# Reordering the first loads, the memory loads and the first branch steps of a one-core hybrid decoder layer

## The chip, the core and the metric

The kernel runs on one core of a Trainium2 chip (trn2). The metric is the device time of one execution in microseconds (us). The engines are PE (TensorE; PEld is its weight load), DVE (VectorE), ACT (ScalarE), POOL (GpSimd) and SP (SyncE, which here only issues DMAs). ACT and POOL can issue DMAs as well.

## What is computed

One decoder layer on 256 tokens of width 1024, in f32. The reference, cut to what matters:

```python
h = rms_norm(x, g_mix)
u_ssm, q, k, v, qi, ki, wi, qm, gates = split(h @ w_in)
km, vm = split(rms_norm(mem, g_mem) @ w_mem_kv)
y_ssm = s5_branch(u_ssm, ...)          # diagonal state space layer, gelu, glu
y_dsa = dsa_branch(q, k, v, qi, ki, wi, pos)   # indexer, top 64 keys per query, attention
y_mem = memory_branch(rms_norm(qm), rms_norm(km), vm)   # cross-attention to mem
merged = g_s * (y_ssm @ w_up_ssm) + g_d * (y_dsa @ w_up_dsa) + g_m * (y_mem @ w_up_mem)
x = x + merged @ w_out
x = x + hier_moe(rms_norm(x, g_ffn), ...)   # 32 experts, two per token
```

## The kernel before, in words

There are two stages. The **dense stage** holds everything up to the output projection. The **expert stage** goes through all 32 experts, each with three weight matrices of 2 MiB.

The dense stage is a list of jobs, each a product of all tokens with a weight matrix of up to 512 columns. A job is cut into *quarters* of two 128-row pieces of the weight. There are 70 quarters; `job` (from L208) appends them in the order of the calls: u (quarters 0 to 3), a (4 to 7), q (8 to 11), then the memory jobs km (12 to 15), qm (16 to 19), vm (20 to 23), the six gates (24 to 47), the up-projections of the memory, of the attention, the GLU, the up-projection of the state space branch, and the output projection. In the code u feeds the state space branch, a and q feed the attention, km, qm and vm the cross-attention.

For each quarter q:

- `load_quarter` (L222 to L227) issues the weight load on SP into one of four raw places; the load of quarter q + 4 therefore has to wait until quarter q is split.
- `split` (L229 to L243) writes the weight as a sum of two fp32r parts: `S.copy` on ACT (L241) makes the high part and `V.tensor_tensor` on DVE (L242) the low one. Quarter 0 is split in two halves, the others in one piece. Then it loads quarter q + 4. The main loop calls `split(q + 2)`.
- `product` (L245 to L264) issues 12 matmuls, each high x high, high x low and low x high (L257, L258, L259), in two parts of six. The last quarter of a job ends with the job's evacuation (`scaled`, L268 to L271, is the one for u, a, q, km, qm, vm: ACT scales by the reciprocal root mean square rx or rm).

The activations are split in the same way by `split_T` (L350 to L354): ACT makes the scaled high part (L353), DVE the low part (L354), in eight pieces of 256 columns, for x from `xT_raw` and for the memory from `mT_raw`.

The three branches are Python generators, "a" (`attention`), "s" (`ssm`) and "m" (`memory`). The table STEPS (L40) has one entry for each half of a quarter, and each letter in it lets that generator issue its next step. A generator that needs a job's result yields the job; its letters then wait until the job is done. `finish` (from L1001) runs a generator until it ends or meets such a wait. "m" may not start before `load_memory` has been called.

The order in which the code is traced is not the final one. A list scheduler with a timing model puts the instructions of each engine, and the DMA issues of SP, in an order of its own; program order is its priority, and `tc.high_priority()` lifts what stands in it (the splits and quarter loads do). Each engine then runs its list strictly in order.

In the kernel before, all first loads are issued by SP: g8 (the norm gains, L193), x^T in three pieces (L194, L332, L334), the quarters, the two halves of x by tokens (L337), `early` (constants, L383), `ssm_bc` (state space matrices, L1064 at q == 1), the positions (L1066, L1067 at q == 2). `load_memory` (L342 to L348) is called at q == 6; it issues both memory loads, memT and mem, of 1 MiB each. Two copies of one column (L345, L346) from u's result tie these loads to the evacuation of job u.

The experts' weights go through a ring of places in SBUF. Most of these places hold data of the dense stage first, and `feed` (L972) issues an expert's load on SP as soon as its place has been given up.

Of the kernel before, what the change touches and what calls it, by code (L numbers as in the profile page):

```python
# [15 lines left out]
AF = mybir.ActivationFunctionType  # L16
# [22 lines left out]

STEPS = ("||s|s|s||sa|a|saa||s|ss|s|s|mm|mm|samm|amm|samm|amm|sa|a|sa|a|sa|a|sa|a|sa|a|sa|a|sam|am|sam|a|sa|a|"  # L40
         "sa|a|sam|am|sam|a|sa|a|sa|a|sam|a|sam|a|sam|a|sam|a|sam|a|sam|a|sam|a|sam|a|sam|a|sam|a|sam|a|sam|a|"
# [30 lines left out]
def hybrid_kernel(ctx: ExitStack, tc: tile.TileContext, A: dict, out: bass.AP):  # L72
# [15 lines left out]
    g8 = pool.tile([128, 2, 8], F32, name="g8")  # L88
# [103 lines left out]

    SP.dma_start(g8, A["g8"])  # L193
    SP.dma_start(xT_raw[:, 0:2], A["xT"][:, 0:2])  # L194

    warm = sl(24, 0, 512).bitcast(BF16)
    G.memset(warm, 0.0)

    S.activation(warm[:, 512:513], warm[:, 0:1], AF.Copy, scale=1.0)
    wps = at()  # L200
# [28 lines left out]
    def split(q):  # L229
        if q >= len(quarters):  # L230
            return
        j, i = quarters[q]
        load_quarter(q)
        w = j["w"]
        src = raw(q).rearrange("p k w -> p (k w)")
        new(SPL[q % 3], F32R)
        hi, lo = (sl(SPL[q % 3], 1024 * n, 2 * w) for n in range(2))
        j["w2"][i] = [v.rearrange("p (k w) -> p k w", k=2) for v in (hi, lo)]
        with tc.high_priority():
            for c in ((slice(0, w), slice(w, 2 * w)) if q == 0 else (slice(0, 2 * w),)):  # L240
                S.copy(hi[:, c], src[:, c])  # L241
                V.tensor_tensor(lo[:, c], src[:, c], hi[:, c], ALU.subtract)  # L242
            load_quarter(q + 4)  # L243
# [64 lines left out]
    Jm_ = dict()  # L308
    for n in ('km', 'qm', 'vm'):
        Jm_[n] = job(n, *(dict(km=(mT, halves(A["w_km"]), 512, scaled(toks[0], rm)), vm=(mT, halves(A["w_vm"]), 512, scaled(vm, rm)),  # L310
                               qm=(hT, halves(A["w_qm"]), 512, scaled(toks[2], rx)))[n]))
# [18 lines left out]

    load_quarter(0)
    SP.dma_start(xT_raw[:, 2:4], A["xT"][:, 2:4])  # L332
    load_quarter(1)
    SP.dma_start(xT_raw[:, 4:8], A["xT"][:, 4:8])  # L334
    load_quarter(3)
    for tt in range(2):
        SP.dma_start(x_tok[:, tt], A["x"][128 * tt:128 * tt + 128])  # L337
    posr, posc = sl(23, 256, 256).bitcast(I32), sl(23, 512, 2).bitcast(I32)
    bre, bim, cre, cim = (sl(21, 256 * i, 256, g=16, h=16) for i in range(4))

    mem_there = dict(done=False)
    def load_memory():  # L342
        mem_there["done"] = True

        S.copy(mT_raw[:, 0, 0:1], toks[0][:, 1, 0:1])  # L345
        S.copy(mem_tok[:, 0, 0:1], toks[0][:, 1, 0:1])  # L346
        for dst, src in ((mT_raw, A["memT"]), (mem_tok, A["mem"].rearrange("(t p) d -> p t d", p=128))):
            SP.dma_start(dst, src)  # L348

# [30 lines left out]
    for n_, _ in enumerate(split_T(hT, xT_raw, g8[:, 0])):  # L380
        if n_ in (1, 3):
            split(n_ // 2)
    SP.dma_start(early, A["early"])  # L383
    with tc.high_priority():
# [458 lines left out]

    def memory():
        sumsq(rm, mem_tok)
        yield
        inv_sqrt(rm, D)
        yield
        yield from split_T(mT, mT_raw, g8[:, 1])
        for J, tok, dst, g in ((Jkm, toks[0], kmT, "gkm"), (Jqm, toks[2], qmT, "gqm")):  # L850
            yield J
# [198 lines left out]
    for q in range(len(quarters)):  # L1050
        j, i = quarters[q]
        if j is Jkm and i == 0:
            finish(mmt)
# [8 lines left out]
        split(q + 2)  # L1062
        if q == 1:
            SP.dma_start(sl(21, 0, 1024), A["ssm_bc"])  # L1064
        if q == 2:
            SP.dma_start(posr, A["pos_row"])  # L1066
            SP.dma_start(posc, A["pos_col"])  # L1067
        if q == 6:
            load_memory()
        for part in range(2):  # L1070
            product(q, part)
            steps(STEPS[2 * q + part])
# [419 lines left out]
```

## Time and profile before

| | |
|---|---|
| median of three runs | 732.78 us (731.33, 732.78, 732.97) |
| profiled execution | 733.47 us |
| its span in the trace | 731.70 us |
| around the span | 1.77 us |
| PE busy | 581.6 us, 79% |
| DVE busy | 308.0 us, 42% |
| ACT busy | 211.5 us, 29% |
| moved by DMA | 246.78 MB, mean 337 GB/s |

The shares are means over two stages that have little in common; they have to be read stage by stage. A time in the trace is counted from the start of the span.

### The profile page before, as it was taken

To read this page: it belongs to the slowest core of one execution; us is meant where nothing else is said; L and a number is where in the kernel's file an instruction comes from. 1 tells how busy PE (TensorE), PEld (TensorE's weight loads), DVE (VectorE), ACT (ScalarE), POOL (GpSimd) and SP (SyncE) were. 2 spreads that over 40 slices of the span, in tenths; PEclk is the share of its full clock that TensorE was granted. 3 is DMA by queue.
4 is the path that set the end of the run, shared out by engine and by line. 5 is a ranking of instruction groups with operands and counts; after the bars stand their busy time and mean duration, and the time that the engine had idled before them with its cause. 6 is when DMAs were issued, how large, how long until landed. Compare 5 with 4: busy or idle time off the path is not lost.

```text
span 731.7 us, 12785 instructions
## 1 busy us (share of the span) xinstructions
PE 581.6 (79%) x5284; PEld 374.3 (51%) x5284; DVE 308.0 (42%) x772; ACT 211.5 (29%) x426; POOL 77.5 (11%) x122
## 2 busy tenths in 40 slices
PE   8889999999998999888676685495577668469765
PEld 4677787786876786444343252252233324234423
DVE  5999999999574755222120021021111012001102
ACT  6776764648743452111100001000000000000002
POOL 2722201001022001202020020001002002000000
PEclk9999999999999999999996799789879789789989
DMA  8874334436757979999999999999999999999992
GB/s 313 317 217 143 125 118 135 144 118 227 276 175 286 320 299 402 428 425 419 431 424 422 430 428 422 428 427 421 429 426 425 427 426 421 429 426 425 420 409 105
DMA packets 31358, 246.78 MB, mean 337 GB/s; under 512 B 3904, under 2 KB 4544, under 8 KB 15936
## 3 DMA queue, kind: packets, MB, share of 16 engines
q1 hardware_dynamic: 30352, 244.87, 83.4%
q8 instruction: 43, 0.70, 0.4%
q0 software_dynamic: 512, 0.53, 0.3%
q10 hardware_dynamic: 432, 0.52, 0.2%
q14 instruction: 19, 0.16, 0.1%
HBM read 244.33 MB, written 1.05 MB: 335 GB/s over the span
## 4 chain that ended last, share of the span: by engine, by line


## 5 line engine op out<-in xcount | busy, mean ns | idle before, releaser
L1267 PE MATMUL w<-arena 128*32 128x256 f32 x1088 | 125.1, 456 | 43.0 <-DMA arena<-w_up 31.0
L1267 PE MATMUL w<-s,arena 128*32 128x256 f32 x960 | 111.8, 439 | 30.7 <-DMA s<-w_up 29.6
L258 PE MATMUL pj<-s,s 128*128 128x512 f32 (+1 forms) x280 | 112.5, 402 | 4.8 <-DVE s L242 4.8
L257 PE MATMUL pj<-s,s 128*128 128x512 f32 (+1 forms) x280 | 110.0, 405 | 7.0 <-ACT s L241 3.4
L259 PE MATMUL pj<-s,s 128*128 128x512 f32 (+1 forms) x280 | 110.3, 397 | 0.1
L1267 PEld LDWEIGHTS w<-arena 128*32 128x32 f32 x1088 | 55.5, 130 | 90.0 <-DMA arena<-w_up 37.1
L242 DVE TENSOR_TENSOR s<-arena,s 128x1024 fp32r<-128x1024 f32 (+2 forms) x71 | 87.0, 1230 | 21.5 <-ACT s L241 20.9
L241 ACT CAST s<-arena 128x1024 fp32r<-128x1024 f32 (+2 forms) x71 | 72.7, 1029 | 47.3 <-PE pj L259 27.6
L1267 PEld LDWEIGHTS w<-s,arena 128*32 128x32 f32 x960 | 50.5, 125 | 69.0 <-DMA s<-w_up 35.8
L1225 POOL TENSOR_SCALAR s<-early,s 128x32 f32<-128x32 f32 x64 | 32.3, 522 | 350.0 <-PE w L1231 295.6
L1324 DVE COPY arena<-w 32x256 f32<-32x256 f32 x62 | 25.9, 418 | 91.4 <-PE w L1319 78.2
L1324 ACT COPY arena<-w 32x256 f32<-32x256 f32 x62 | 22.5, 364 | 143.7 <-DVE arena L1324 143.7
L257 PEld LDWEIGHTS pj<-s,s 128*128 128x128 f32 x280 | 52.4, 189 | 21.8 <-ACT s L241 6.7
L258 PEld LDWEIGHTS pj<-s,s 128*128 128x128 f32 x280 | 53.1, 190 | 18.8 <-DVE s L242 8.5
L1305 DVE TENSOR_TENSOR early<-w,early 64x256 f32<-64x256 f32 x16 | 6.8, 428 | 126.9 <-ACT early L1304 126.9
L259 PEld LDWEIGHTS pj<-s,s 128*128 128x128 f32 x280 | 53.0, 190 | 10.5 <-DVE s L696 0.5
L1304 ACT ACTIVATE misc<-w 64x256 f32<-64x256 f32 x16 | 6.0, 375 | 137.0 <-PE w L1267 137.0
L1319 PE MATMUL w<-s,s 128*32 128x256 f32 x544 | 34.8, 397 | 10.4 <-DVE s L1310 6.1
L1319 PE MATMUL w<-arena,s 128*32 128x256 f32 x448 | 32.2, 434 | 9.5 <-DMA arena<-w_down 6.0
L1304 ACT ACTIVATE early<-w 64x256 f32<-64x256 f32 x16 | 6.0, 377 | 115.6 <-PE w L1267 115.6
L1305 DVE TENSOR_TENSOR misc<-w,misc 64x256 f32<-64x256 f32 x16 | 6.8, 426 | 72.6 <-ACT misc L1304 72.6
L1260 DVE TENSOR_TENSOR arena<-w,misc 128x256 f32<-128x256 f32 x32 | 12.1, 420 | 57.1 <-PE w L1257 57.1
(307 smaller groups left out, 690.0 us busy)
## 6 DMA issues: line engine op xcount, KB each, us to landing
arena<-w_up SPq DMA_DIRECT2D x15, 2048.0 KB, 29.5
arena<-w_gate SPq DMA_DIRECT2D x13, 2048.0 KB, 29.5
arena<-w_down SPq DMA_DIRECT2D x12, 2048.0 KB, 30.7
s<-w_down SPq DMA_DIRECT2D x12, 2048.0 KB, 31.9
s<-w_gate SPq DMA_DIRECT2D x11, 2048.0 KB, 34.3
s<-w_up SPq DMA_DIRECT2D x9, 2048.0 KB, 34.2
s<-w_up SPq DMA_DIRECT2D x13, 1024.0 KB, 27.1
arena<-w_g SPq DMA_DIRECT2D x24, 512.0 KB, 3.9
```

The costliest lines, as they stand in the source:

```text
L241: S.copy(hi[:, c], src[:, c])
L242: V.tensor_tensor(lo[:, c], src[:, c], hi[:, c], ALU.subtract)
L257: PE.matmul(ps, lhsT=lh, rhs=hi[:, k], start=kt == 0, stop=False)
L258: PE.matmul(ps, lhsT=lh, rhs=lo[:, k], start=False, stop=False)
L259: PE.matmul(ps, lhsT=ll, rhs=hi[:, k], start=False, stop=kt == j["kts"] - 1)
L1225: G.tensor_scalar(dst[:, tt, :], iota[:, 0:CAP], col[:, tt:tt + 1], fac[:, tt:tt + 1], ALU.is_equal, ALU.mult)
L1260: V.tensor_tensor(xe[:, h], xg[:, k:k + 2], b_(gff[:, h], 128), ALU.mult)
L1267: PE.matmul(gu[32 * q:32 * q + 32, :], lhsT=xe[:, kt, 32 * j:32 * j + 32], rhs=w[:, kt % 4, 256 * (q % 2):256 * (q % 2) + 256], start=kt = ...
L1304: S.activation(sg[64:128, :], gu[0:64, :], AF.Silu)
L1305: V.tensor_tensor(hid, gu[64:128, :], sg[64:128, :], ALU.mult)
L1319: PE.matmul(dn[32 * q:32 * q + 32, :], lhsT=hd[:, kb, 32 * c:32 * c + 32], rhs=w[:, kb, 256 * q:256 * q + 256], start=c + kb == 0, stop=c ...
L1324: (S.copy if q % 2 else V.tensor_copy)(Y[32 * j:32 * j + 32, 256 * q:256 * q + 256], dn[32 * q:32 * q + 32, :])
```

## The change

It has seven edits.

1. SP's DMA issues stand in program order until quarter 11 (`manual_schedule`, closed at q == 11). After that the scheduler orders them again.
2. x^T pieces 0:2 and 2:4 and g8 are issued by ACT, in the order x^T 0:2, g8, x^T 2:4. SP begins with the two pieces of quarter 0, then quarter 1, x^T 4:8, quarters 2 and 3 and the first half of x; the second half of x follows quarter 4's load, `early` quarter 5's.
3. The warming activation on ACT (L199) is traced at high priority, and quarter 1 is split in two halves as quarter 0 is.
4. `ssm_bc` is loaded at q == 3 instead of q == 1. The positions stay at q == 2; in SP's program order they stand behind the load of quarter 8, `ssm_bc` behind that of quarter 9.
5. `load_memory` is called at q == 8 (memT) and at q == 11 (mem), and the two copies of one column are gone.
6. Job qm comes ahead of km (quarters 12 to 15 and 16 to 19), and "m" treats the queries first. "m" scales memT before it sums the squares of mem.
7. STEPS: the first "s" step moves from the first half of quarter 1 to the second half of quarter 2, the first "a" step from the first half of quarter 3 to the second half of quarter 4, the first "m" step from the first half of quarter 7 to the first half of quarter 10. From the second half of quarter 15 on, all three generators stand where they stood.

```diff
-STEPS = ("||s|s|s||sa|a|saa||s|ss|s|s|mm|mm|samm|amm|samm|amm|sa|a|sa|a|sa|a|sa|a|sa|a|sa|a|sam|am|sam|a|sa|a|"
+STEPS = ("|||||s|s|s||sa|a|saa||s|ss|s|sa|sa|sa|a|sam|am|sam|am|samm|am|samm|am|sam|am|sa|a|sam|am|sam|a|sa|a|"
...
-    SP.dma_start(g8, A["g8"])
-    SP.dma_start(xT_raw[:, 0:2], A["xT"][:, 0:2])
+    first = ExitStack()
+    first.enter_context(tc.manual_schedule(engines={mybir.EngineType.SP}))
+    S.dma_start(xT_raw[:, 0:2], A["xT"][:, 0:2])
+    S.dma_start(g8, A["g8"])
+    S.dma_start(xT_raw[:, 2:4], A["xT"][:, 2:4])
...
-    S.activation(warm[:, 512:513], warm[:, 0:1], AF.Copy, scale=1.0)
+    with tc.high_priority():
+        S.activation(warm[:, 512:513], warm[:, 0:1], AF.Copy, scale=1.0)
...
-            for c in ((slice(0, w), slice(w, 2 * w)) if q == 0 else (slice(0, 2 * w),)):
+            for c in ((slice(0, w), slice(w, 2 * w)) if q < 2 else (slice(0, 2 * w),)):
...
-    for n in ('km', 'qm', 'vm'):
+    for n in ('qm', 'km', 'vm'):
...
-    load_quarter(0)
-    SP.dma_start(xT_raw[:, 2:4], A["xT"][:, 2:4])
     load_quarter(1)
     SP.dma_start(xT_raw[:, 4:8], A["xT"][:, 4:8])
     load_quarter(3)
-    for tt in range(2):
-        SP.dma_start(x_tok[:, tt], A["x"][128 * tt:128 * tt + 128])
+    SP.dma_start(x_tok[:, 0], A["x"][0:128])
...
     def load_memory():
+        if not mem_there["done"]:
+            SP.dma_start(mT_raw, A["memT"])
+        else:
+            SP.dma_start(mem_tok, A["mem"].rearrange("(t p) d -> p t d", p=128))
         mem_there["done"] = True
-        S.copy(mT_raw[:, 0, 0:1], toks[0][:, 1, 0:1])
-        S.copy(mem_tok[:, 0, 0:1], toks[0][:, 1, 0:1])
-        for dst, src in ((mT_raw, A["memT"]), (mem_tok, A["mem"].rearrange("(t p) d -> p t d", p=128))):
-            SP.dma_start(dst, src)
...
         if n_ in (1, 3):
             split(n_ // 2)
+            if n_ == 1:
+                SP.dma_start(x_tok[:, 1], A["x"][128:256])
...
     def memory():
+        yield from split_T(mT, mT_raw, g8[:, 1])
         sumsq(rm, mem_tok)
         yield
         inv_sqrt(rm, D)
         yield
-        yield from split_T(mT, mT_raw, g8[:, 1])
-        for J, tok, dst, g in ((Jkm, toks[0], kmT, "gkm"), (Jqm, toks[2], qmT, "gqm")):
+        for J, tok, dst, g in ((Jqm, toks[2], qmT, "gqm"), (Jkm, toks[0], kmT, "gkm")):
...
-        if j is Jkm and i == 0:
+        if j is Jqm and i == 3:
             finish(mmt)
...
-        if q == 1:
+        if q == 3:
             SP.dma_start(sl(21, 0, 1024), A["ssm_bc"])
...
-        if q == 6:
+        if q in (8, 11):
             load_memory()
+        if q == 11:
+            first.close()
```

## Rows read from the trace of the kernel before

**Rows 1.** Busy time by stretch of the span; x is the number of instructions.

```profile
core 0: us, PE busy (x) PEld busy (x) DVE busy (x) ACT busy (x) POOL busy (x), PEclk, DMA share, GB/s
6.20:42.00 35.80, 29.68 (x125) 22.13 (x126) 32.04 (x100) 28.81 (x54) 17.69 (x22) 1.00 0.87 318
17.09:182.00 164.91, 158.66 (x1156) 124.71 (x1155) 162.50 (x440) 109.94 (x217) 31.33 (x33) 1.00 0.53 173
42.00:180.00 138.00, 137.19 (x1063) 108.59 (x1063) 136.60 (x351) 87.59 (x175) 13.64 (x12) 1.00 0.47 150
182.00:228.00 46.00, 43.30 (x264) 34.73 (x263) 27.22 (x54) 26.21 (x48) 6.42 (x12) 1.00 0.62 209
228.00:285.00 57.00, 54.18 (x262) 43.68 (x260) 35.16 (x56) 24.82 (x36) 3.57 (x3) 0.97 0.90 342
285.00:700.00 415.00, 293.86 (x3343) 154.10 (x3345) 69.18 (x196) 34.85 (x93) 32.28 (x64) 0.88 1.01 425
```

**Rows 2.** PE in order of time to 46 us; brackets: idle before, its releaser.

```profile
6.20 0.73 PE L257 MATMUL pj<-s,s 128*128 128x512 f32 x2 [0.69 <-ACT s L241]
10.16 0.73 PE L257 MATMUL pj<-s,s 128*128 128x512 f32 x2 [0.66 <-ACT s L241]
...
11.42 0.51 PE L258 MATMUL pj<-s,s 128*128 128x512 f32 x1 [0.53 <-DVE s L242]
...
22.30 1.06 PE L257 MATMUL pj<-s,s 128*128 128x452 f32 x2 [1.43 <-ACT s L241]
...
31.72 0.47 PE L258 MATMUL pj<-s,s 128*128 128x452 f32 x1 [1.14 <-DVE s L242]
...
37.61 0.50 PE L257 MATMUL pj<-s,s 128*128 128x512 f32 x1 [1.07 <-ACT arena L270]
...
40.32 0.50 PE L258 MATMUL pj<-s,s 128*128 128x512 f32 x1 [0.82 <-DVE s L242]
...
44.09 0.39 PE L257 MATMUL pj<-s,s 128*128 128x512 f32 x1
44.32 0.39 PE L258 MATMUL pj<-s,s 128*128 128x512 f32 x1
```

**Rows 3.** Waits of PE from 180 to 290 us: total, times, longest.

```profile
PE pj L257 <- ACT s L724: 1.6, 2, 1.1
```

**Rows 4.** DMA issues of SP in order of time.

```profile
1.19 0.41 SPq L194 DMA_DIRECT2D s<-xT  x1
1.66 0.90 SPq L226 DMA_DIRECT2D arena<-w_u  x2
...
3.07 0.43 SPq L226 DMA_DIRECT2D arena<-w_u  x1
...
13.33 2.89 SPq L226 DMA_DIRECT2D arena<-w_a  x3
```

**Rows 5.** ACT in order of time.

```profile
4.73 0.91 ACT L353 ACTIVATE s<-s,g 128x256 fp32r<-128x256 f32 x2 [2.51 <-DMA s<-xT]
...
9.06 1.04 ACT L241 CAST s<-arena 128x1024 fp32r<-128x1024 f32 x1 [0.36 <-DMA arena<-w_u]
...
31.74 3.31 ACT L353 ACTIVATE s<-s,g 128x256 fp32r<-128x256 f32 x8 [1.42 <-DMA s<-memT]
```

**Rows 6.** Two early stretches, columns as in rows 1.

```profile
5.00:7.00 2.00, 1.31 (x5) 0.37 (x3) 1.70 (x4) 1.67 (x4) 0.00 (x0) 1.00 0.64 207
7.00:9.00 2.00, 2.00 (x9) 1.65 (x10) 1.14 (x3) 0.91 (x2) 0.00 (x0) 1.00 1.02 412
5.28:17.09 11.81, 9.93 (x40) 6.85 (x39) 8.32 (x13) 9.38 (x17) 0.00 (x0) 1.00 0.97 379
```

**Rows 7.** DVE in order of time.

```profile
18.05 1.09 DVE L242 TENSOR_TENSOR s<-arena,s 128x904 fp32r<-128x904 f32 x1
```

**Rows 8.** DMA issues by form: KB each, us from issue to landing.

```profile
s<-memT SPq DMA_DIRECT2D x1, 1024.0 KB, 7.2
...
arena<-pos_row SPq DMA_DIRECT2D x1, 128.0 KB, 9.1
```

## The prediction, made before the change was run

> **What bounds the kernel now.** I begin with the busy times by stretch, because shares over the whole span mix two stages. From 285 to 700 us the DMA engines are full (share 1.01, 425 GB/s) while PE is busy 293.86 of 415 us [rows 1]. The expert stage is bound by its weights. Nothing of the change touches it, so its length stays; it can only begin earlier or later, namely when the dense stage gives up the places of the ring. A microsecond won or lost at about 285 us is a microsecond of the whole.
>
> In the dense stage the reader should see two full engines, not one. From 42 to 180 us PE is busy 137.19 of 138 us and DVE 136.60 [rows 1]. DVE is full over a longer stretch: 162.50 of 164.91 us from 17.09 to 182 us. From 182 to 228 us DVE has 27.22 of 46 us of work and PE 43.30, so there PE sets the pace, with a few waits for the attention's end: 1.6 us of products that waited for L724, the splitting of a branch's output [rows 3]. From 228 to 285 us PE is busy 54.18 of 57 us.
>
> The early part is different. From its first product at 6.20 us to 42 us PE is busy 29.68 of 35.80 us, so 6.12 us are idle [rows 1]. The timeline of PE gives six stalls that hold 5.65 of them: 0.66 and 0.53 at quarter 1, 1.43 at 22.30, then 1.14, 1.07 and 0.82 between 31 and 41 us [rows 2]. The change works on this part alone: by the step table all three generators stand, from the second half of quarter 15 on, where they stood.
>
> **The change part by part.** I keep two accounts, since two engines are full: what PE gains, and what DVE gains.
>
> *Start.* x^T's first piece moves from SP's second place (issued at 1.19 us) to the first of ACT's queue, the first weight pieces from 1.66 us to SP's first place [rows 4]. Each issue ahead took about 0.4 us, so x^T wins 0.4 us and the weight 0.9. ACT first acts on x^T at 4.73 us after waiting 2.51 us for it [rows 5]; three issues of 0.41 us fit into that wait. The first product needs both loads, so it gains between 0.4 and 0.9 us; I take 0.6, the x^T being what ACT waited for. Both engines gain it. g8 behind x^T: small, inside the same wait. The high priority of the warming activation and the second half-split of quarter 1 are costed at nothing, as ACT waits there anyway; without that wait a half-split costs an instruction's start, under 0.1 us.
>
> *Fill of the first transfers.* From 5 to 7 us the DMA engines were busy to 0.64 and moved 207 GB/s; from 7 to 9 us it was 1.02 and 412 GB/s [rows 6]. By 4 us SP had issued, by the order and shapes in the code, 2 MB [rows 4], and at 9.06 us ACT still waited for the last of it but one [rows 5], so the queue was not empty. If a second queue filled that dip, everything behind it would land 2 x (412 - 207) / 412 = 1.0 us earlier. The bounds are 0 and 1.0; I take 0, as no row shows two queues at once and the dip came with work outstanding. [...]
>
> *Quarter 1.* Its load is issued at 3.07 us [rows 4] and ACT splits it at 9.06 us after 0.36 us of waiting for it [rows 5]. It goes to SP's third place, 1.4 us earlier, but with the same bytes ahead of it. Of the stalls of 0.66 and 0.53 us I count half, 0.6 us; bounds 0 and 1.2.
>
> *Quarter 5 ahead of the constants.* At 13.33 us begin the loads of w_a's later quarters, behind `early`, `ssm_bc` and the positions, which by their shapes in the code are together about 0.96 MB: at 412 GB/s that is 2.3 us of transfers that now come behind them. The 1.43 us stall at 22.30 hangs on that split [rows 2]. I count it as gone for PE. What is late next is the evacuation of job u: it needs the sums of squares of x, whose second half is now issued behind quarter 4's load. So PE may meet a wait of up to 1.4 us in the same place; half is taken back, 0.7 us.
>
> *Branch steps and memory out of the first 42 us.* The three stalls between 31 and 41 us, 3.03 us together [rows 2], come while ACT scales the memory in one block of 3.31 us [rows 5] and DVE takes its half of that and the first branch steps. Moving them behind later quarters frees PE: bounds 0 and 3.03, I take 2.5. For DVE nothing is saved; the same instructions are issued, with both memory loads, between quarters 10 and 15, when PE is full. The two removed copies of one column are ACT instructions of 0.2 us at most: nothing, ACT is idle 7 of these 35.8 us [rows 1]. The order of qm and km changes no shape and no count: nothing, hidden by the full PE.
>
> *The fixed order of SP.* Each quarter's load waits for a raw place, and all behind it waits too. memT now stands behind the load of quarter 14, thus behind the split of quarter 10; its landing took 7.2 us [rows 8]. Its first scaling is traced two and a half quarters later. A product is 0.23 us [rows 2], a quarter of twelve 2.7 us, so 6.8 us: about the landing. Before, ACT waited 1.42 us for the same load [rows 5]. I take this wait as equal, bounds 0 and 1.4 more.
>
> **The sum.** PE's account: 0.6 + 0.6 + 0.7 + 2.5 = 4.4 us; its upper bound is 6.12 + 0.6 = 6.7. DVE's account: from its first instruction at 5.28 us to 17.09 us DVE is busy 8.32 of 11.81 us [rows 6], and from then on full to 182 us. Its later work is the same, so it ends earlier only by what is pulled into these 3.49 idle us: the earlier start, 0.6, and the split of quarter 4, 1.09 us [rows 7], which should come before 17.09 us instead of after. That is 1.7 us. The end lies between the accounts. After 182 us PE sets the pace, which is for PE's lead of 4.4; but the attention's last step waits for what DVE finishes at 182 us, and PE already waits there, which is for 1.7. I take **2.8 us**, nearer the DVE account, since DVE is full longer. The profiled execution has 733.47 us, 0.69 over the median of 732.78. Against its own time the sum gives 730.7, against the median 730.0 us, which is the forecast.
>
> **The rivals.** A measurement of this kernel can tell about 0.3%, 2.2 us, from no change.
>
> *The whole of PE's lead is kept.* The static order after 182 us places products where PE would wait, and the three stalls and that of quarter 5 vanish: 6.12 + 0.6 less the evacuation's 1.07 [rows 2] is 5.6 us, 727.2. For it speaks that DVE is half idle after 182 us; against it that DVE is full for 165 us before.
>
> *No change that can be measured.* DVE alone decides, and quarter 4's split isn't pulled ahead because its load lands as before: only the start is left, 0.6 to 1 us, 731.8. For it speaks DVE's stretch of 162.50 of 164.91 us; PE would arrive 4 us early and wait for the branches. Here also falls the case that the second queue changes no landing at all.
>
> *Slower, by an empty DVE.* Place: DVE from 17 to about 28 us. It was full there because branch steps were ready. Now they begin one and a half quarters later, 4.1 us, and the positions, whose landing took 9.1 us [rows 8], stand behind the load of quarter 8, which waits for quarter 4's split (18.05 us before, [rows 7]). If nothing but splits is ready for DVE in that time, up to 4.1 us of its full stretch move to the back, and DVE ends 4.1 - 1.7 = 2.4 us later: 735.2. It decides from the point where more than 1.7 us of DVE's time stay empty between the first product and quarter 10. Against it: ACT and PE are the ones that DVE waited for early, and the constants in `early` alone feed a good part of the first "s" step.
>
> **How the numbers follow.** The forecast's own case, 1.7 to 4.4 us, has a chance of 0.48; the whole lead 0.14; no change 0.24; slower 0.14. Of the forecast's case 0.10 lies under 2.2 us. So faster by over 0.3% has 0.38 + 0.14 = 0.52, within 0.3% 0.24 + 0.10 = 0.34, slower 0.14. The range goes from PE's upper bound, 732.78 - 6.7 = 726.1, cut to 726.5, up to the slower rival's 735.2. The forecast's own range is 728.4 to 731.1. The new static order is one more unknown, as the scheduler places everything anew; the ends between 182 and 228 us may move by a microsecond or two either way, and the range holds that too.
>
> **What would show it.** The first product at about 5.6 us. PE idle under 3 us from its first product to 42 us, where it was 6.12, with no stall at the fifth quarter's split and none of the three between 31 and 41 us. DVE's full stretch ends near 180 us. The products' wait for L724 grows by one or two microseconds, since PE comes earlier than the attention. The full DMA stretch begins near 282 us and is as long as before. The prediction is wrong if DVE shows idle time between 17 and 40 us, if ACT waits longer than 1.4 us for memT or mem, or if PE's gain is whole at 42 us and gone at 228.

## The result and the profile after

The changed kernel takes 738.91 us (median of 13 runs, 734.87 to 742.59) against 732.78 us: a ratio of 1.0094, 95% interval 1.0082 to 1.0107. It is 6.1 us slower, and no case of the prediction but the slower rival had that sign. The profiled execution has 738.28 us, its span is 736.5 us, 4.8 longer than the span of the kernel before. A profile is one execution: this one took 0.63 us less than the median, that of the kernel before 0.69 more.

I read the windows first. This is the busy time by stretch of the changed kernel, with the columns of [rows 1].

```profile
6.20:42.00 35.80, 33.52 (x148) 28.15 (x149) 32.35 (x103) 28.59 (x48) 16.02 (x23) 0.95 0.83 294
17.09:182.00 164.91, 158.15 (x1142) 125.64 (x1141) 159.42 (x428) 103.22 (x196) 27.26 (x31) 0.99 0.51 167
42.00:180.00 138.00, 132.34 (x1021) 103.67 (x1020) 134.63 (x333) 82.59 (x163) 11.14 (x9) 0.99 0.46 149
182.00:228.00 46.00, 43.08 (x253) 34.42 (x252) 28.33 (x61) 30.24 (x65) 8.43 (x13) 0.96 0.58 205
228.00:285.00 57.00, 53.25 (x255) 42.50 (x254) 34.16 (x39) 23.55 (x32) 4.80 (x3) 0.97 0.84 318
285.00:700.00 415.00, 294.16 (x3325) 155.81 (x3323) 72.70 (x215) 37.90 (x100) 32.43 (x64) 0.90 1.01 425
```

The expert stage is as before. Its first product starts at 295.8 us instead of 290.2, and from there to the end of the span it is 440.7 us, before 441.5. So the loss is 5.6 us of the dense stage, less 0.8 in the expert stage, and the place where the dense stage ends decides the time.

Up to 42 us the change did most of what it was meant to: PE is idle 2.28 us where it was 6.12 [rows 1], and the products of quarter 12 begin at 43.0 us instead of 48.2. From 42 to 180 us this turns round: PE is idle 5.66 us instead of 0.81, DVE 3.37 instead of 1.40. Counted in PE's order, twelve to a quarter, the products of quarter 16 begin only 1.2 us earlier than before, those of quarter 22 already 1.5 us later (85.5 against 84.1).

The 5.6 us can be added up on PE, which has the same matmuls to do in both kernels. From the first product to the first product of the experts (the kernel before first, then the changed one):

```profile
6.20:290.20 284.00, 269.90 (x1740) 212.46 (x1740) 235.81 (x582) 171.18 (x317) 43.24 (x52) 0.99 0.64 226
7.38:295.79 288.41, 273.50 (x1740) 217.41 (x1740) 238.07 (x584) 171.46 (x317) 42.41 (x52) 0.98 0.62 221
```

The first product comes 1.2 us later. PE is idle 14.91 us instead of 14.10, 0.8 more: the idle time won before 42 us came back later. And PE is busy 3.6 us longer with as many matmuls. So the largest part of the loss stands in no idle time; what differs there is the granted clock (0.98 against 0.99, read in stretches below). This sum says where PE's time went and not what caused it.

DVE is the other full engine. From 17.09 to 182 us it is idle 5.49 us of 164.91 instead of 2.41. The last instruction of the search for the top keys ends at 185.1 us instead of 182.2, 2.9 us later, but this is not that idle time alone: it stands in DVE's list behind an instruction that waits 2.36 us for ACT, mostly behind 182 us.

```profile
184.70 0.18 DVE L713 RECIPROCAL misc<-misc 128x4 f32<-128x4 f32 x1 [2.36 <-ACT arena L711]
```

Nor does the end of the search set the end of the dense stage, as three of the experiments show.

Where PE waits, its timeline shows. These are the stalls of the changed kernel that the text goes back to (brackets: idle before, its releaser), in the form of [rows 2].

```profile
7.38 0.73 PE L262 MATMUL pj<-s,s 128*128 128x512 f32 x2 [2.06 <-ACT s L354]
...
30.16 0.47 PE L263 MATMUL pj<-s,s 128*128 128x452 f32 x1 [1.10 <-DVE s L247]
...
50.26 0.73 PE L262 MATMUL pj<-s,s 128*128 128x512 f32 x2 [1.23 <-ACT s L246]
52.73 0.79 PE L262 MATMUL pj<-s,s 128*128 128x512 f32 x1 [1.74 <-ACT s L246]
...
185.66 1.38 PE L262 MATMUL pj<-s,s 128*128 128x512 f32 x2 [2.50 <-ACT s L246]
...
245.70 0.50 PE L262 MATMUL pj<-s,s 128*128 128x512 f32 x1 [1.81 <-ACT s L698]
```

Of the stalls of [rows 2] the one at 22.30 us is gone, and of the three between 31 and 41 us the two at 37.61 and 40.32. The third, 1.14 us at 31.72, stayed: it is the 1.10 us at 30.16, in the same quarter and for the same step of DVE. Three new places matter: the first product, the stalls at 50 to 53 us, that at 186 us. ACT releases all three, so ACT's timeline is next. First the start (L246 makes a weight's high part, L354 scales an activation):

```profile
1.17 0.46 ACTq L197 DMA_DIRECT2D g<-g  x1
...
5.80 0.62 ACT L246 CAST s<-arena 128x512 fp32r<-128x512 f32 x1 [2.63 <-DMA arena<-w_u]
6.82 0.91 ACT L354 ACTIVATE s<-s,g 128x256 fp32r<-128x256 f32 x2 [0.41 <-DMA g<-g]
```

ACT scales the first x^T at 6.82 us, before at 4.73 [rows 5], and the last thing it waits for is g8, the 8 KB of norm gains. The DMA issues by form say why (KB each, us from issue to landing; the kernel before first, then the changed one):

```profile
s<-xT SPq DMA_DIRECT2D x2, 256.0 KB, 4.3
g<-g SPq DMA_DIRECT2D x1, 8.0 KB, 1.7
```

```profile
s<-memT SPq DMA_DIRECT2D x1, 1024.0 KB, 9.2
s<-xT ACTq DMA_DIRECT2D x2, 256.0 KB, 6.1
g<-g ACTq DMA_DIRECT2D x1, 8.0 KB, 5.6
```

Behind x^T on ACT's queue and beside SP's weights, g8 lands after 5.6 us instead of 1.7, and x^T after 6.1 instead of 4.3.

Then the memory, in ACT's timeline of the changed kernel, and the wait that follows on DVE:

```profile
45.97 3.31 ACT L354 ACTIVATE s<-s,g 128x256 fp32r<-128x256 f32 x8 [3.23 <-DMA s<-memT]
49.18 1.03 ACT L246 CAST s<-arena 128x1024 fp32r<-128x1024 f32 x1
...
50.70 1.98 ACT L246 CAST s<-arena 128x1024 fp32r<-128x1024 f32 x2
...
57.05 1.05 ACT L246 CAST s<-arena 128x1024 fp32r<-128x1024 f32 x1 [1.65 <-PE pj L264]
```

```profile
58.12 1.23 DVE L247 TENSOR_TENSOR s<-arena,s 128x1024 fp32r<-128x1024 f32 x1 [1.86 <-ACT s L246]
```

This is one chain, and the reader can follow it line by line. memT is issued at 36.74 us (before at 24.55) and lands 9.2 us later, just ahead of 45.97, where ACT goes on. ACT stands still for it for 3.23 us and then scales for 3.31; the casts of the next quarters' weights are behind that in its list. So PE waits for L246 at 50.26 and 52.73, then runs at half clock (below), so ACT waits 1.65 us for PE at 57.05, and DVE 1.86 us for ACT at 58.12. One late load stopped three engines in turn. (That the half clock makes ACT's second wait is read from the order in time.)

The last column to read is the granted clock. In four stretches of the changed kernel it is about half:

```profile
8.00:12.00 4.00, 4.00 (x12) 3.14 (x11) 3.71 (x8) 3.56 (x9) 0.00 (x0) 0.57 1.03 423
52.00:56.00 4.00, 3.27 (x8) 2.59 (x9) 3.94 (x10) 3.36 (x6) 0.00 (x0) 0.57 0.68 220
185.00:189.00 4.00, 3.34 (x8) 2.46 (x9) 3.08 (x7) 3.78 (x9) 1.03 (x1) 0.58 0.15 46
247.00:251.00 4.00, 4.00 (x12) 3.15 (x11) 0.57 (x1) 0.00 (x0) 0.00 (x0) 0.57 0.97 413
```

In the kernel before there is one, behind the stall of 1.35 us at 232.85:

```profile
233.00:238.00 5.00, 5.00 (x16) 3.91 (x16) 2.22 (x2) 1.05 (x1) 0.94 (x1) 0.66 1.01 419
```

Each of the four follows one of the longer stalls above, and each holds 0.43 x 4 = 1.7 us of lost clock (0.34 x 5 = 1.7 before). That would be 5.1 us more than before where PE is busy 3.6 longer; PE is idle for a part of two of the stretches, and the rest of the difference is not explained. Products stand 0.43 us apart there (187.26, 187.69, 188.12) instead of 0.23 (189.25, 189.48). From 8 to 12 us PE shows as busy for 4.00 of 4.00 us, with 12 products at a clock of 0.57, so such a loss stands in no idle time.

### The profile page after: what moved, and what is told of

Same layout as the page of the kernel before. It is cut to its first block, busy times and chain, and to the rows that moved or that the text cites. A ratio compares the mean times of both kernels' runs of the same rounds, so it can differ in the third digit from the quotient of the medians.

```text
span 736.5 us, 12776 instructions
## 1 busy us (share of the span) xinstructions
PE 582.1 (79%) x5284; PEld 377.7 (51%) x5284; DVE 310.1 (42%) x773; ACT 211.6 (29%) x425; POOL 76.9 (10%) x122
## 3 DMA queue, kind: packets, MB, share of 16 engines
HBM read 244.33 MB, written 1.05 MB: 333 GB/s over the span
## 4 chain that ended last, share of the span: by engine, by line
## 5 line engine op out<-in xcount | busy, mean ns | idle before, releaser
L1272 PE MATMUL w<-arena 128*32 128x256 f32 x1088 | 122.2, 445 | 42.4 <-DMA arena<-w_up 35.4
L247 DVE TENSOR_TENSOR s<-arena,s 128x1024 fp32r<-128x1024 f32 (+2 forms) x72 | 89.9, 1252 | 30.1 <-ACT s L246 29.8
L246 ACT CAST s<-arena 128x1024 fp32r<-128x1024 f32 (+2 forms) x72 | 72.4, 1016 | 49.6 <-PE pj L264 28.7
L262 PEld LDWEIGHTS pj<-s,s 128*128 128x128 f32 x280 | 53.5, 193 | 23.4 <-ACT s L246 7.0
L263 PEld LDWEIGHTS pj<-s,s 128*128 128x128 f32 x280 | 54.1, 193 | 14.7 <-DVE s L247 4.0
L264 PEld LDWEIGHTS pj<-s,s 128*128 128x128 f32 x280 | 54.2, 194 | 10.7 <-issue 0.2
```

Of the source, the lines that this page charges most:

```text
L262: PE.matmul(ps, lhsT=lh, rhs=hi[:, k], start=kt == 0, stop=False)
L263: PE.matmul(ps, lhsT=lh, rhs=lo[:, k], start=False, stop=False)
L264: PE.matmul(ps, lhsT=ll, rhs=hi[:, k], start=False, stop=kt == j["kts"] - 1)
L1272: PE.matmul(gu[32 * q:32 * q + 32, :], lhsT=xe[:, kt, 32 * j:32 * j + 32], rhs=w[:, kt % 4, 256 * (q % 2):256 * (q % 2) + 256], start=kt = ...
```

## The experiments

"Dense end" is the start of the first expert product: 290.2 us in the kernel before, 295.8 in the changed one. All ratios are to the kernel before, on the same chip.

**The changed kernel with g8 first.** The order of all other engines stays.

```diff
-    S.dma_start(xT_raw[:, 0:2], A["xT"][:, 0:2])
     S.dma_start(g8, A["g8"])
+    S.dma_start(xT_raw[:, 0:2], A["xT"][:, 0:2])
```

> The changed kernel with g8 issued ahead of x^T on ACT; every other instruction stands in the same order on every engine. Theory A (waits and the clock behind them add up): the first product, at 7.38 us in the changed kernel, moves to about 6.0, the stretch of half clock from 8 to 12 us goes, and the end comes 2 to 3 us earlier, about 736.3. Theory B (DVE, full until 182 us, and the static order behind it decide, so early waits of PE are swallowed): under 1 us, 738 to 739.

It took 739.88 us (736.96 to 742.48), 1.0121 [1.0100, 1.0141]. Its profile is that of a further execution, of 739.25 us:

> The kernel with g8 first once more, for an undisturbed profile: its times (739.88 median) showed no gain. Theory B says that the first product comes at about 6.0 us without the half clock at 8 to 12 us, and that the lead is gone by 110 us in waits for DVE; theory A would need the first product to be as late as before.

PE's timeline in that profile:

```profile
6.83 1.22 PE L262 MATMUL pj<-s,s 128*128 128x512 f32 x2 [1.07 <-ACT s L354]
7.85 1.05 PE L263 MATMUL pj<-s,s 128*128 128x512 f32 x2
...
52.12 0.80 PE L262 MATMUL pj<-s,s 128*128 128x512 f32 x1 [1.74 <-ACT s L246]
184.96 0.80 PE L262 MATMUL pj<-s,s 128*128 128x512 f32 x1 [2.51 <-ACT s L246]
```

The stall ahead of the first product halves. The half clock at the start did not go, though: the second row has two products in 1.05 us, and they stand 0.43 us apart until 10.4 us. So the products are only 0.3 us ahead up to quarter 13, then 0.6 to 0.7 (dense end 295.2). The stalls of 1.74 and 2.50 us are the same within a hundredth. So g8's place is worth about 0.6 us of the 6, less than the spread of the runs; the rest is elsewhere, and what the half clock at the start is worth this run does not tell.

**Memory loaded earlier: at quarters 6 and 9, and at 4 and 6.**

```diff
-        if q in (8, 11):
+        if q in (6, 9):
```

> The changed kernel with memT loaded at quarter 6 and mem at quarter 9 instead of 8 and 11. Theory A: ACT's wait of 3.23 us for memT goes, with PE's stalls of 1.23 and 1.74 us at 50 to 53 us and the half clock behind them; 4 to 5 us earlier, about 734.5. Theory B: PE idles less at 50 us but the end moves by under 2 us either way, 737 to 741, since the waits from 180 us on stay or others come.

739.88 us, 1.0111 [1.0094, 1.0128]: nothing gained. The scaling of memT was put earlier as well, at 42.73 us, and ACT still waited 2.37 us for the load. Moving the load was no remedy here, as its first user moved with it.

```diff
-        if q in (8, 11):
+        if q in (4, 6):
```

> The changed kernel with memT loaded at quarter 4 and mem at quarter 6, so that both have landed long before their first use. Theory A' (the changed kernel's 5.6 us of later dense stage are PE's long stalls and the half clock behind each): no wait of ACT for memT, no stall of PE and no half clock near 50 us; 2 to 5 us under the changed kernel, 734 to 737. Theory B' (the static order after 60 us decides alone): the stall near 50 us goes and stalls of the same sum come later, 738 to 742.

736.72 us (734.67 to 737.25), 1.0054 [1.0033, 1.0074]. Here ACT scales memT without a wait, at 32.05 and 34.31 us, and from 42 to 180 us PE is busy 134.87 us instead of 132.34 and DVE 136.59 instead of 134.63. The loss falls from 0.94% to 0.54%, so the late memory carries two to three microseconds of it. It is not the wait alone that was taken away: the scaling stands 12 to 14 us earlier too, and with it the order on PE, DVE and ACT is another from about 30 us on. The dense end (294.9) moves by 0.9 only, as this order has its own stalls, 1.63 us at 175.96 and these:

```profile
192.38 0.66 PE L721 MATMUL mm<-early,s 128*128 128x128 f32 x4 [2.12 <-ACT s L722]
221.46 1.09 PE L830 MATMUL at<-arena,misc 128*64 128x128 f32 x14 [1.56 <-ACT arena L722]
```

**Both repairs: g8 first and memory at quarters 4 and 6.** The edits are the first and the last diff above together.

> The changed kernel with g8 first and the memory loads at quarters 4 and 6. Theory A': both early stalls are gone, 1 us or more under the kernel with the memory loads alone, 732 to 736. Theory B': 737 to 742.

734.06 us (732.07 to 736.63), 1.0035 [1.0020, 1.0051], dense end 291.2: of the loss of 0.94%, 0.35% is left. The windows show why nothing is won beyond that:

```profile
17.09:182.00 164.91, 160.61 (x1169) 129.06 (x1168) 161.46 (x431) 106.92 (x206) 30.93 (x32) 1.00 0.54 175
182.00:228.00 46.00, 40.47 (x242) 31.84 (x240) 27.60 (x55) 26.84 (x56) 6.93 (x13) 0.96 0.52 179
228.00:285.00 57.00, 53.52 (x263) 43.06 (x263) 36.35 (x55) 24.67 (x36) 4.77 (x3) 1.00 0.91 348
```

By 182 us PE has done 1.95 us more than before [rows 1] and has no wait for memT. Then it is idle 9.01 us up to 285 us, 3.5 more than before. Its longest waits there are for the memory branch, 2.12 us at 191.44 and 0.72 at 193.17, then 1.55 us for the attention at 219.69 and 1.48 for a weight's low part at 234.81. A lead of PE alone is spent there.

The two kernels with memory at quarters 4 and 6 differ by g8's place only; all instructions behind it stand in one order. Yet the dense end with g8 first is 3.7 us earlier. Two stretches, with g8 second and then with g8 first:

```profile
193.00:200.00 7.00, 6.53 (x28) 6.06 (x28) 2.34 (x9) 1.62 (x3) 0.00 (x0) 0.52 0.99 398
223.00:228.00 5.00, 4.77 (x15) 3.56 (x16) 1.14 (x3) 0.00 (x0) 1.54 (x4) 0.66 0.00 0
```

```profile
193.00:200.00 7.00, 6.83 (x38) 6.37 (x39) 2.47 (x11) 1.28 (x5) 0.00 (x0) 0.76 0.91 368
223.00:228.00 5.00, 5.00 (x36) 3.82 (x34) 1.13 (x1) 3.28 (x5) 0.00 (x0) 1.00 0.43 105
```

Its products are 0.7 us ahead at quarter 44 (169 us), no more than at the first product, and 3.7 at quarter 56 (233 us). In between the longer stalls of the two are alike (2.12 us near 192 us, 1.56 and 1.55 near 220), and the clock accounts for the rest: by these rows it loses 0.24 x 7 + 0.34 x 5 = 3.4 us less. So the half clock behind 182 us went into the end almost whole in this pair. It is one profile of each; the medians differ by 2.7 us, and the ranges overlap.

**Half of the change: the loads (edits 1 to 4) without the steps, and the steps (edits 5 to 7) without the loads.** The first, in the kernel before:

```diff
+    first.enter_context(tc.manual_schedule(engines={mybir.EngineType.SP}))
+    S.dma_start(xT_raw[:, 0:2], A["xT"][:, 0:2])
+    S.dma_start(g8, A["g8"])
+    S.dma_start(xT_raw[:, 2:4], A["xT"][:, 2:4])
...
+        if q == 3:
             SP.dma_start(sl(21, 0, 1024), A["ssm_bc"])
```

> The kernel before with only the edits of the first loads (SP's fixed order, ACT's three issues, quarter 1 in halves, ssm_bc at quarter 3); steps, memory and its jobs as before. Theory A: the late first product and the half clock at 8 to 12 us stay (about 3 us), memT is not late: 735 to 736. Theory B: 731 to 735, whatever PE loses before 40 us being covered by DVE's full stretch.

741.81 us, 1.0138 [1.0121, 1.0155], dense end 297.9: the loads alone are worse than the whole change, and neither theory had this. memT is late here too: SP issues it at 32.02 us, it lands 10.6 us later, and ACT waits 2.37 us for it, the casts behind it. PE's longest stalls are 3.20 us at 48.13, 2.70 at 205.81 and 2.69 at 73.58. ACT's wait:

```profile
42.66 3.30 ACT L355 ACTIVATE s<-s,g 128x256 fp32r<-128x256 f32 x8 [2.37 <-DMA s<-memT]
```

The second, in the kernel before:

```diff
-        if q == 6:
+        if q in (8, 11):
             load_memory()
...
-    for n in ('km', 'qm', 'vm'):
+    for n in ('qm', 'km', 'vm'):
...
+STEPS = ("|||||s|s|s||sa|a|saa||s|ss|s|sa|sa|sa|a|sam|am|sam|am|samm|am|samm|am|sam|am|sa|a|sam|am|sam|a|sa|a|"
```

> The kernel before with only the step table, the memory loads at quarters 8 and 11, the queries ahead of the keys and the step order in memory; the first loads and SP's free order as before, by which the scheduler puts memT behind the positions. Theory A: memT is there early, no wait for it, the first product at 6.2 us, PE's lead of some 4 us is kept: 728 to 731. Theory B (the moved branch steps themselves make the later order worse): 735 to 739.

735.14 us, 1.0035 [1.0019, 1.0051], the time that theory B named, but what the trace shows is late weights and not the moved steps. Without the fixed order the scheduler issues memT at 13.21 us and mem at 15.80, ahead of weights that are needed sooner, though the program names them later. PE stalls for those weights:

```profile
29.62 0.68 PE L257 MATMUL pj<-s,s 128*128 128x452 f32 x2 [3.28 <-ACT s L241]
33.36 0.75 PE L258 MATMUL pj<-s,s 128*128 128x452 f32 x1 [3.06 <-DVE s L242]
```

From 6.20 to 42 us PE is busy only 26.31 us, 3.4 less than before [rows 1], and at a granted clock of 0.86. Yet the dense end is 290.5 us, 0.3 later than before, and the span 733.4 us, 1.7 longer. In this profile most of what PE loses early does not arrive at the end of the dense stage, as most of what the changed kernel wins early does not.

**The fixed order by itself.** The changed kernel without it, then the kernel before with nothing else.

```diff
-    first.enter_context(tc.manual_schedule(engines={mybir.EngineType.SP}))
```

> The changed kernel with SP's issues left to the scheduler again (no manual_schedule); all other edits stay. Theory C (SP's fixed order is what costs, since the loads of the constants and the memory come late and the order of the other engines is then off): close to the steps-only kernel, 733 to 736. Theory D (the three issues on ACT cost, through the late g8 and the late first product): no better than the changed kernel, 737 to 741.

743.39 us, 1.0146 [1.0129, 1.0163], worse than either theory. memT is issued at 13.90 us here, and one stall of PE is 5.52 us:

```profile
35.10 1.12 PE L261 MATMUL pj<-s,s 128*128 128x452 f32 x2 [5.52 <-ACT s L245]
```

```diff
+    first = ExitStack()
+    first.enter_context(tc.manual_schedule(engines={mybir.EngineType.SP}))
...
+        if q == 11:
+            first.close()
```

> The kernel before with only manual_schedule on SP until quarter 11; loads, steps and memory as before, all first loads on SP. Theory C: 737 to 742, as the loads-only kernel's 741.8. Theory D: 731 to 734, no change.

735.20 us, 1.0042 [1.0027, 1.0057], between the two theories. So the fixed order by itself costs about 3 us in the kernel before and saves about 4 in the changed one. The parts do not add: loads +10 us, steps +3, the whole +6.

These runs also answer whether the end of the search sets the dense end. It ends at 175.8 us with the steps alone, 174.2 in the changed kernel without the fixed order and 173.8 with the fixed order alone, 6 to 8 us earlier than before; the dense ends are 290.5, 300.7 and 291.4 us, none earlier. The search's last instruction in the second of them:

```profile
173.92 0.28 DVE L790 TENSOR_SCALAR arena<-arena 128x256 f32<-128x256 f32 x1
```

**First loads on ACT alone**, in the kernel before: x^T 0:2, g8, x^T 2:4; then the same with g8 first.

```diff
-    SP.dma_start(g8, A["g8"])
-    SP.dma_start(xT_raw[:, 0:2], A["xT"][:, 0:2])
+    S.dma_start(xT_raw[:, 0:2], A["xT"][:, 0:2])
+    S.dma_start(g8, A["g8"])
+    S.dma_start(xT_raw[:, 2:4], A["xT"][:, 2:4])
```

> The kernel before with only x^T 0:2, g8 and x^T 2:4 issued by ACT; SP's order free. Theory C: 731 to 734. Theory D: 735 to 740, with a first product later than 7 us.

730.52 us, 0.9973 [0.9960, 0.9985], although here too g8 is late (PE waits 1.96 us at 7.72 us) and behind 60 us products stand 0.2 us later than in the kernel before. What differs is the clock from 233 to 238 us, behind the same stall of 1.35 us: full, and the dense end is 288.8.

> The kernel with ACT's three issues alone, g8 first. Its orders on DVE and SP are those of the kernel with x^T first, on PE and ACT nearly. First product near 6.0 us instead of 7.72, no half clock after it. If an early lead is kept: 728.5 to 730. If DVE's full stretch swallows it: 730 to 731.5, no change from that kernel's 730.52.

730.29 us (730.02 to 731.76), 0.9976 [0.9967, 0.9985], dense end 287.3; it beats both kernels, by 1.8 us the one before. Its row for that stretch, against 0.66 above:

```profile
233.00:238.00 5.00, 4.75 (x25) 3.75 (x24) 2.62 (x3) 2.24 (x3) 0.00 (x0) 1.00 0.96 401
```

Its search ends at 180.9 us, 1.3 earlier than before, and with 1.7 us of clock that is the 2.9 us of the dense end. Its time lies in the range named for a swallowed lead (730 to 731.5); in the profile the lead is kept, 1.4 us at quarter 10 and 1.3 at quarter 50. That the kernel before loses its 1.7 us of clock in every execution is not shown, and the medians differ by less than the 2.9.

**Is DVE's full stretch what sets the end?** The kernel before with four instead of eight rounds of the search in each half. It leaves out half of the search.

```diff
-            for _ in range(8):
+            for _ in range(4):
```

> The kernel before with four rounds of the top-64 search instead of eight in each of the two halves (it leaves out half of the search): 8 pairs of MAX8 and MATCH_REPLACE8 less on DVE, 8 x 0.8 = 6 us of DVE's full stretch and nothing on PE. If DVE's full stretch sets the end of the dense stage: 4 to 6 us faster, 727 to 729. If PE sets it: under 1.5 us either way, 731 to 734.

730.29 us, 0.9974 [0.9964, 0.9983]. DVE is busy 5.3 us less from 17.09 to 182 us (157.22 instead of 162.50), and the whole is 1.9 us shorter, between the two cases. Now PE is full behind 182 us, 45.76 of 46 us:

```profile
182.00:228.00 46.00, 45.76 (x273) 36.90 (x269) 28.86 (x55) 25.61 (x47) 8.23 (x13) 1.00 0.68 244
```

DVE is not the bound alone; take its work away and PE is, within 2 us.

**Does the half clock carry the loss?** Three kernels on one chip: the changed kernel with five more warming matmuls, meant to fill PE's gap ahead of the first product; the same with memory at quarters 4 and 6; and the changed kernel again.

```diff
-    for _ in range(9):
+    for _ in range(14):
```

> The changed kernel with fourteen instead of nine warming matmuls; every other instruction of every engine stands in the same order. In the changed kernel the ninth ends at 5.33 us, PE is then idle for 2.06 us to its first product at 7.38, and from 8 to 12 us the granted clock is 0.5, which costs 1.71 us. Theory clock: what a wait of PE costs here is the wait and the half clock behind it; with the gap filled the clock from 8 to 12 us is full, the first product still starts at 7.4, products are 1.7 us ahead at quarter 4, and if DVE is not the bound there the attention's end and the dense end come 0.5 to 1.7 us earlier: 737.2 to 738.4. Rival DVE: products are 1.7 us ahead at quarter 4 and no lead is left at quarter 16, the dense end stays at 295.8 +- 0.5 and the time at 738.9. Rival no effect: the half clock at 8 to 12 us stays, so it does not come from the gap.

> The changed kernel with memory loaded at quarters 4 and 6, with fourteen warming matmuls in place of nine. The same run with nine took 736.72 us, dense end at 294.9, half clock at 8 to 12, 193 to 200 and 223 to 228 us; with g8 first as well 734.06 us and one half-clock stretch. Theory clock: the stretch at 8 to 12 us goes and the lead of 1.7 us reaches quarter 10; whether the two late stretches go too depends on the stalls at 176 to 222 us, so 733.5 to 736. Rival start: it was the earlier first product, not the clock, that made the repaired kernel faster, and the time stays at 736.7.

> The changed kernel itself once more, beside the two others on one chip: 738.9 us within 0.3 per cent; half clock at 8 to 12, 52 to 56, 185 to 189 and 247 to 251 us if these stretches belong to the order of the instructions, at other places if they are chance.

The first took 739.15 us, 1.0099 [1.0084, 1.0115], the changed kernel again 741.05 us, 1.0118 [1.0100, 1.0136]; the intervals overlap. With fourteen matmuls the clock from 8 to 12 us is full (1.00 and 18 products, where the row above has 0.57 and 12) and the products are 1.7 us ahead at quarter 1, but 0.4 from quarter 3 on and 0.2 from quarter 14 on, and the dense end is 296.0. So the clock lost at the start cost nothing at the end here; my theory, that each stretch costs its 1.7 us, fell for this one. The rival had the end right and the place wrong: the lead is gone by quarter 3. What takes it is shown in part only, by a stall of 0.53 us for DVE at 14.44. The second took 734.91 us, 1.0033 [1.0020, 1.0046], against 1.0054 [1.0033, 1.0074] with nine; its dense end is 294.5 against 294.9, too little to tell.

The changed kernel again shows half clock at other places with the same instructions:

```profile
52.00:56.00 4.00, 3.69 (x9) 2.92 (x10) 3.94 (x9) 3.04 (x6) 0.00 (x0) 0.50 0.60 175
56.00:59.00 3.00, 3.00 (x10) 2.36 (x9) 1.18 (x5) 1.04 (x1) 0.00 (x0) 0.60 0.79 284
239.00:243.00 4.00, 4.00 (x12) 3.13 (x11) 1.63 (x1) 0.00 (x0) 0.55 (x1) 0.57 0.97 373
```

The stretch at 52 us is longer, and the last one is at 239 instead of 247 us. At the start the column must not be trusted: from 8 to 12 us it shows 1.00, but the products stand there 0.43 us apart until 10.6 us, two in 1.05 us:

```profile
8.00:12.00 4.00, 4.00 (x13) 3.11 (x13) 3.70 (x8) 3.55 (x9) 0.00 (x0) 1.00 1.02 416
```

```profile
8.53 1.05 PE L263 MATMUL pj<-s,s 128*128 128x512 f32 x2
```

The row has 13 products, where the changed kernel's first profile has 12 at 0.57 and the one with fourteen warming matmuls 18 at 1.00. Why the column shows 1.00 there no run tells. Quarter 16 begins 0.9 us later than in the first profile, and this keeps to the dense end (296.9 against 295.8). So the longer stretch in the middle did cost, about one microsecond here. Where the clock falls was not the same in these two profiles of one kernel (247 us in the first, 239 in the second). The spread of the changed kernel's runs, 7.7 us where the kernel before has 2.1, would fit that; the link is my estimate from the two profiles and not shown.

## Why the prediction was wrong

The early part was right in kind: the stall of quarter 5 and two of the three of the branch steps are gone (the third, 1.14 us, is 1.10 now), PE's idle time before 42 us falls under 3 us, and 5.2 us of lead at quarter 12 are more than PE's account of 4.4. The reading that the expert stage only starts earlier or later held to 0.8 us. What failed, step by step:

- **"The fixed order of SP"** is the step that failed, as far as one could be singled out. I took ACT's wait for memT as equal, with at most 1.4 us more. It rose from 1.42 to 3.23 us, more than even that bound, since the landing took 9.2 us, where I took 7.2, and there were 6.0 us between its issue and its user, where I had 6.8. Worse, I priced the wait alone. Behind it in ACT's list stood casts of weights for a PE without slack, and the wait went on to PE (1.23 and 1.74), to the clock, back to ACT (1.65) and to DVE (1.86). Memory at quarters 4 and 6 took two to three microseconds of the loss of six away; as its scaling moved as well, the share of the wait by itself is not shown.
- **"The new static order"** was given "a microsecond or two either way". This was sized too small: parts of the change alone moved the time by +10 us (loads), +3 (steps) and +3 (the fixed order), and the change without the fixed order by +11. Which line of the order costs what stays open.
- **"Start"** was taken at a gain of 0.6 us; the first product came 1.2 us later (7.38 instead of 6.20). "g8 behind x^T: small" was wrong: its landing rose from 1.7 to 5.6 us. x^T landed later as well, so with g8 first the product still came at 6.83. At the end this is worth 0.6 us (first experiment). A half-split by itself is under 0.1 us on ACT, as taken: in the kernel before, two halves at 5.55 us take 1.12 us together, a whole piece at 12.01 takes 1.04.
- **"Fill of the first transfers"**: the dip did fill. From 5 to 7 us the changed kernel's DMA engines are busy to 1.00 at 361 GB/s, against 0.64 and 207 [rows 6], and with the first loads on ACT as the sole edit to 1.02 at 358. I took 0, as no row shows two queues at once and the dip came with work outstanding; that was an estimate, and it fell. The first small loads landed later all the same (x^T after 6.1 instead of 4.3 us, g8 after 5.6 instead of 1.7). Whether it filled because more was issued sooner or because two queues ran, no run here tells.
- **"Branch steps and memory out of the first 42 us"**: the claim that DVE and PE take the moved steps later at no cost failed. From 42 to 180 us both had been full; there PE's idle time rose from 0.81 to 5.66 us and DVE's from 1.40 to 3.37.
- **The sum** had no term for the clock. PE is busy 3.6 us longer with as many matmuls; from 182 to 228 us alone the clock fell from 1.00 to 0.96, 1.8 us. The row of the kernel before at 0.97 from 228 to 285 [rows 1] had been there to ask about.
- **The rival "Slower, by an empty DVE"** had the sign, and a part of its mechanism came true. In its place DVE did stand idle more, though it got busier ahead of that (9.46 us from 5.28 to 17.09, before 8.32 [rows 6]). The kernel before first:

```profile
17.00:40.00 23.00, 18.39 (x82) 13.95 (x80) 22.62 (x83) 18.43 (x38) 15.81 (x19) 1.00 0.86 301
17.00:40.00 23.00, 21.90 (x105) 18.69 (x104) 20.98 (x82) 17.41 (x30) 14.03 (x19) 1.00 0.72 237
```

  That is 2.02 us instead of 0.38. About as much again came behind 42 us, where the longest wait is at 58.12, at the end of memT's chain. Its mark of 1.7 us does not decide: from the first product to quarter 10 DVE was idle for longer than that in the kernel before too (3.76 us, now 2.98). Its price, 2.4 us by a later end of DVE's work, was near the 2.9 us of the search by luck, since the end of the search does not set the end. And it left out the clock.
- Of the signs of being wrong all three came true: DVE idle between 17 and 40 us, ACT's wait for memT over 1.4 us, and PE's gain whole at 42 us and gone at 228. The products' wait for the splitting of a branch's output did not grow; waits for the casts took its place (2.50 us at 185.66). There ACT runs the gelu between two groups of exp with a table load each (1.28 us at 178.94 and at 181.30), and the weight's cast comes only at 184.58; in the kernel before one table load stands in that stretch.

Whether PE's or DVE's account sets the end was the wrong question: the repaired kernel gains on PE and hands it back, half a search less on DVE gives 1.9 of 5.3 us, and a search that ends 6 to 8 us earlier gives nothing. Of the last 0.35% of loss in the repaired kernel I know the place (PE's waits behind 182 us, the longest for the memory branch) and not which line of the order makes them. How much of the 6 us the half clock behind 42 us carries stays open: between two kernels of one order it made about 3 us, but no kernel takes it away and leaves the rest of the changed kernel as it is.

## What to carry to other kernels

Before moving a load later, list what stands behind its first user on that engine's queue, and take the landing from where the load will be issued, not from where it was (memT took 7.2 us to land at its old place, 9.2 at the new one). In the stretch here, where PE and DVE had been full, ACT's wait of 3.23 us was passed on to PE (1.23 and 1.74) and to DVE (1.86). When several queues issue the first loads, issue the small one that everything waits for first (worth 0.6 us here). Read the granted clock beside the idle time, and look at the distance of the products where the clock's column is in doubt (0.43 us instead of 0.23 under a column of 1.00). Time each part of a change by itself: here the whole cost 6 us, and a piece of one edit of the seven alone won 2.

## What the runs showed of the hardware

I had not expected the clock to fall behind stalls this short. In the dense stage of the profile of the kernel before and of the changed kernel's first, each fall of the granted clock came behind an idle time of PE: of 1.35 us at 232.85 in the kernel before (0.66 from 233 to 238 us), of 2.06, 1.74, 2.50 and 1.81 in the changed one (0.57 to 0.58 in the four stretches). But the same stall of 1.35 us at 233.06 was followed by a full clock (1.00 from 233 to 238 us) when only the first loads were issued elsewhere, and two profiles of one kernel differ in the places. Nor did I expect that the column of the clock can show 1.00 for products 0.43 us apart, as at the start of the changed kernel's second profile, nor that a load of 8 KB took 5.6 us to land behind x^T on ACT's queue, where it took 1.7 as the first of SP's.
